# Gated GELU on one core: 8-row tiles with packed output buffers, against 16-row blocks stored from the first load's buffer

## The chip, the core and the metric

The kernel runs on one core of a Trainium2 chip. Of the core's engines three matter here: ScalarE (ACT in the profile) evaluates the GELU, VectorE (DVE) multiplies, and SyncE (SP) computes nothing but issues transfers. ACT issues transfers too. Each of the two has its own queue for them (q1 is SP's, q10 is ACT's in the profile), and both queues are served by the same 16 DMA engines. The metric is device time in microseconds; lower is better. The kernel before was run three times: 469.32, 469.19 and 469.43 us, median 469.32.

## What is computed

```python
def reference(x):                      # x: (32, 512, 2048) float32
    half_dim = x.shape[-1] // 2
    x1, x2 = (x[..., :half_dim].copy(), x[..., half_dim:].copy())
    gelu_x1 = 0.5 * x1 * (1 + erf(x1 / np.sqrt(2)))
    return (gelu_x1 * x2).astype(np.float32)
```

There are 32 x 512 = 16,384 rows of 2048 numbers (8 KB a row). Each gives an output row of 1024 numbers (4 KB). So 134.2 MB are read, 67.1 MB are written, and each element is used once.

## The kernel before, in words

**Tiling.** A tile is 1024 rows: each of the 128 partitions holds R = 8 consecutive rows, so partition p of tile i holds rows 1024 i + 8 p onwards, 64 KB in one piece of DRAM, and its output is 32 KB in one piece (L26 to L29). There are 16 tiles. Two input buffers `x0`, `x1` (64 KB a partition each) and two output buffers `o0`, `o1` (32 KB a partition each) alternate (L30, L31).

**Loads.** All are issued by SP (`load`, L48 to L51). Tile 0 is loaded as two halves of four rows, tile 1 whole; these three wait for nothing (L65 to L69). After tile i has been multiplied, SP issues the load of tile i + 2 into the same input buffer (L113 to L115). It waits only for `mul_done`, not for a store.

**Compute.** For each tile ACT waits until the tile is there (L83, L85), and writes the GELU of the first halves of the rows into the output buffer (L87). DVE waits for ACT and multiplies the output buffer by the second halves, in place (L93 to L100). A tile is done in two steps, rows 0 to 4 and rows 5 to 7; the first and the last tile in three steps of 2, 2 and 4 rows.

**Stores.** ACT issues the store of tile i as soon as DVE has finished it (`store`, L53 to L57); the last two tiles' stores are issued by SP (L105, L110). The load of tile i + 2 and the store of tile i count on one semaphore, `ready[k]`, and ACT waits for both before it overwrites `o[k]`.

**Order.** Everything is written out by hand with counted semaphores. Each queue is a line of its own: what SP issues goes behind what SP issued before, what ACT issues behind what ACT issued before. A small 4 KB transfer to `scrap` opens ACT's queue (L63).

Of the kernel before, what the change touches and what calls it, by code (L numbers as in the profile page):

```python
# [1 line left out]

# [4 lines left out]

GELU = mybir.ActivationFunctionType.Gelu


@with_exitstack
def kernel(
    ctx: ExitStack,
    tc: tile.TileContext,
    x: bass.AP,
    out: bass.AP,
):
    nc = tc.nc
    P = nc.NUM_PARTITIONS

    x_flat = x.flatten_outer_dims()
    out_flat = out.flatten_outer_dims()
    n_rows, dim = x_flat.shape
    half = dim // 2

    R = 8  # L26
    x_t = x_flat.rearrange("(n p r) d -> n p r d", p=P, r=R)
    o_t = out_flat.rearrange("(n p r) d -> n p r d", p=P, r=R)
    n_tiles = x_t.shape[0]  # L29
    x_bufs = [nc.alloc_sbuf_tensor(f"x{k}_tile", [P, R, dim], x.dtype) for k in range(2)]  # L30
    o_bufs = [nc.alloc_sbuf_tensor(f"o{k}_tile", [P, R, half], out.dtype) for k in range(2)]  # L31

    first = [nc.alloc_semaphore(f"first{j}") for j in range(2)]
    ready = [nc.alloc_semaphore(f"ready{k}") for k in range(2)]
    gelu_done = nc.alloc_semaphore("gelu_done")
    mul_done = nc.alloc_semaphore("mul_done")
    tail_stored = nc.alloc_semaphore("tail_stored")
    opened = nc.alloc_semaphore("opened")  # L40
    scrap = nc.alloc_sbuf_tensor("scrap_tile", [8, 128], x.dtype)
    n = {sem.name: 0 for sem in [*first, *ready, gelu_done, mul_done, tail_stored, opened]}

    def counted(ins, sem, by):
        ins.then_inc(sem, by)
        n[sem.name] += by

    def load(i, rows, sem):  # L48
        ins = nc.sync.dma_start(out=x_bufs[i % 2][:, rows, :], in_=x_t[i][:, rows, :])  # L49
        counted(ins, sem, 16)  # L50
        return ins  # L51

    def store(queue, i, rows, sem):  # L53
        queue.wait_ge(mul_done, n[mul_done.name])
        counted(
            queue.dma_start(out=o_t[i][:, rows, :], in_=o_bufs[i % 2][:, rows, :]), sem, 16
        )  # L57

    opening = nc.scalar.dma_start(out=scrap[:, :], in_=x_t[0][:8, 0, :128])  # L63
    counted(opening, opened, 16)
    for ins in (  # L65
        opening,
        load(0, slice(0, 4), first[0]),
        load(0, slice(4, 8), first[1]),
        load(1, slice(0, 8), ready[1]),  # L69
    ):  # L70
        tc.no_tile_sem_insts.add(ins.ins.name)
    tc.close()
    tc.compile()  # L73

    for i in range(n_tiles):
        k = i % 2
        last = i == n_tiles - 1
        pieces = i == 0 or last
        steps = ((0, 2), (2, 4), (4, 8)) if pieces else ((0, 5), (5, 8))
        for lo, hi in steps:  # L80
            rows = slice(lo, hi)
            if i == 0 and lo % 4 == 0:
                nc.scalar.wait_ge(first[lo // 4], 16)  # L83
            elif lo == 0:
                nc.scalar.wait_ge(ready[k], n[ready[k].name])  # L85
            counted(
                nc.scalar.activation(  # L87
                    out=o_bufs[k][:, rows, :], in_=x_bufs[k][:, rows, :half], func=GELU
                ),
                gelu_done,  # L90
                1,
            )
            nc.vector.wait_ge(gelu_done, n[gelu_done.name])  # L93
            counted(
                nc.vector.tensor_mul(  # L95
                    out=o_bufs[k][:, rows, :],
                    in0=o_bufs[k][:, rows, :],
                    in1=x_bufs[k][:, rows, half:],
                ),
                mul_done,  # L100
                1,
            )
            if pieces and hi % 4 == 0:
                if last:
                    store(nc.sync, i, slice(hi - 4, hi), tail_stored)  # L105
                else:
                    store(nc.scalar, i, slice(hi - 4, hi), ready[k])
        if not pieces:
            if i == n_tiles - 2:
                store(nc.sync, i, slice(0, R), tail_stored)  # L110
            else:
                store(nc.scalar, i, slice(0, R), ready[k])
        if i + 2 < n_tiles:  # L113
            nc.sync.wait_ge(mul_done, n[mul_done.name])
            load(i + 2, slice(0, R), ready[k])  # L115


    nc.scalar.wait_ge(opened, 16)
    nc.scalar.drain()  # L119
    for sem in (*first, *ready, opened):  # L120
        nc.scalar.sem_clear(sem)
    nc.vector.drain()
    nc.vector.sem_clear(gelu_done)
    nc.sync.sem_clear(mul_done)
    nc.sync.wait_ge(tail_stored, n[tail_stored.name]).then_inc(
        tail_stored, -n[tail_stored.name]
    )


# [1 line left out]
_INS = ['x']  # L131
_OUTS = [((32, 512, 1024), 'float32')]


# [23 lines left out]
```

## Time and profile before

| what | value |
|---|---|
| median of three runs | 469.32 us (469.19 to 469.43) |
| the profiled execution, first to last event (its span) | 467.8 us |
| what a run's time holds besides (median less span) | 1.5 us |
| DVE busy | 140.5 us, 30% of the span, 34 multiplications |
| ACT busy | 115.5 us, 25%, 34 GELUs and one table load |
| HBM read and written | 134.22 MB and 67.11 MB |
| DMA packets | 5057, mean rate 430 GB/s over the span |

The profiled execution has no time of its own other than its span; the runs of the table were timed around the whole program, 1.5 us more. A duration in the profile is that of one execution. The page's slices cut the span into 40 pieces of 11.7 us, and a digit of 9 in the DMA line means that the 16 DMA engines were busy for 90% of a slice or more. A transfer ("DMA issue") is cut into packets, and the trace records each one's queue, size, start and duration. Here a packet is what one partition gets or gives in one transfer: 64 KB, 32 KB or 16 KB. "Landing" is the time at which a transfer's semaphore has its full count of 16, one from each DMA engine.

### The profile page before, as it was taken

How to read it: one execution, taken by the hardware profiler on the slowest of the kernel's cores; microseconds unless marked ns; L12 is line 12 of the kernel's file. 1: busy time of each engine (PE TensorE's matmuls, PEld its weight loads, DVE VectorE, ACT ScalarE, POOL GpSimd, SP SyncE). 2: the span in 40 equal slices, each digit the busy share in tenths (PEclk: the TensorE clock that was granted, in tenths of full speed). 3: DMA queues.
4: the chain of work that ended last, by engine and by line, in shares of the span. 5: the costliest groups of instructions: out<-in, count | busy, mean ns of one | idle time of the engine just before them, and what ended most of it. 6: DMA issues, size and time to landing. Idle time of an engine off the chain costs nothing.

```text
span 467.8 us, 154 instructions
## 1 busy us (share of the span) xinstructions
DVE 140.5 (30%) x34; ACT 115.5 (25%) x35; POOL 0.2 (0%) x4
## 2 busy tenths in 40 slices
DVE  0330515207051060511606115060150702507043
ACT  1320606041060410604105050050501506014060
POOL 0000000000000000000000000000000000000000
DMA  8999999999999999999999999999999999999988
GB/s 359 448 448 448 398 406 496 403 403 448 459 437 403 440 412 493 403 403 448 487 409 403 445 406 493 403 403 448 493 403 403 448 426 471 403 426 426 493 384 379
DMA packets 5057, 201.34 MB, mean 430 GB/s; under 512 B 568, under 2 KB 576, under 8 KB 576
## 3 DMA queue, kind: packets, MB, share of 16 engines
q1 hardware_dynamic: 2880, 142.61, 70.6%
q10 hardware_dynamic: 2176, 58.73, 29.1%
q14 instruction: 1, 0.01, 0.0%
HBM read 134.22 MB, written 67.11 MB: 430 GB/s over the span
## 4 chain that ended last, share of the span: by engine, by line
DMA 76%; DVE 14%; ACT 8%; ACTq 0%; SPq 0%; issue 0%
DMA out_dram<-o_tile 66%; DVE o_tile L95 14%; DMA x_tile<-in_x_dram 10%; ACT o_tile L87 8%; ACTq L119 0%; SPq L49 0%
## 5 line engine op out<-in xcount | busy, mean ns | idle before, releaser
L95 DVE TENSOR_TENSOR o_tile<-o_tile,x_tile 128x5120 f32<-128x5120 f32 (+3 forms) x34 | 140.5, 4171 | 319.7 <-ACT o_tile L87 319.7
L87 ACT ACTIVATE o_tile<-x_tile 128x5120 f32<-128x5120 f32 (+3 forms) x34 | 114.3, 3407 | 337.3 <-DMA out_dram<-o_tile 301.8
L87 ACT ACT_TABLE_LOAD x1 | 1.3, 1283 | 2.9 <-PEq L73 2.9
L142 POOL MEMSET const-bfloat16-1.0<- 128x1 bf16 x1 | 0.1, 102 | 0.0
L142 POOL MEMSET const-uint8-127<- 128x1 uint8 x1 | 0.1, 101 | 0.0
L142 POOL MEMSET const-float32-0.0<- 128x1 f32 x1 | 0.1, 99 | 0.2 <-issue 0.2
L142 POOL MEMSET const-float32-1.0<- 128x1 f32 x1 | 0.1, 98 | 0.0
## 6 DMA issues: line engine op xcount, KB each, us to landing
out_dram<-o_tile ACTq DMA_DIRECT2D x13, 4096.0 KB, 44.7
x_tile<-in_x_dram SPq DMA_DIRECT2D x2, 4096.0 KB, 16.7
out_dram<-o_tile ACTq DMA_DIRECT2D x2, 2048.0 KB, 34.4
out_dram<-o_tile SPq DMA_DIRECT2D x1, 4096.0 KB, 25.2
out_dram<-o_tile SPq DMA_DIRECT2D x2, 2048.0 KB, 7.8
x_tile<-in_x_dram SPq DMA_DIRECT2D x15, 44.4
scrap_tile<-in_x_dram ACTq DMA_DIRECT2D x1, 4.0 KB
```

The source lines that it names most:

```text
L87: nc.scalar.activation(out=o_bufs[k][:, rows, :], in_=x_bufs[k][:, rows, :half], func=GELU),
L95: nc.vector.tensor_mul(out=o_bufs[k][:, rows, :], in0=o_bufs[k][:, rows, :], in1=x_bufs[k][:, rows, half:],),
L142: nc = _bacc.Bacc("TRN2", target_bir_lowering=False, num_devices=1)
```

## The change: blocks of 16 rows a partition

A block is now 2048 rows, and there are 8 of them. A partition holds a chunk of 16 consecutive rows of the block (128 KB of input, 64 KB of output). The chunk comes in two loads, `h = 0` for its first 8 rows and `h = 1` for its last 8. Each load is 64 KB a partition, as a whole tile was before.

- **Which chunk lies where.** With G = 32 and J = 4, chunk 32 j + g of the block lies in partition 4 g + j. Before, chunk p lay in partition p. So four neighbouring partitions now hold chunks that are 4 MB of input apart, and the next four hold the chunks that follow those.
- **Buffers.** `front[0]` and `front[1]` (64 KB a partition each) take the `h = 0` loads of even and odd blocks; a single `back` (64 KB) takes every `h = 1` load. There is no output buffer.
- **Compute.** ACT writes the GELU over the first halves of the rows, in the buffer in which they were loaded. DVE writes the product packed: that of `h = 0` to the first 32 KB of `front[b % 2]`, over numbers that it has read already, and that of `h = 1`, read from `back`, to the last 32 KB of the same buffer. Before each multiplication DVE now also waits for its own multiplication before that one.
- **Stores.** One store of 64 KB a partition for each block, from `front[b % 2]`, issued by ACT after the block's last multiplication. The last block is stored in three pieces by SP (8, 4 and 4 rows).
- **Loads.** After a block's last multiplication SP issues the `h = 1` load of the next block (`back` is free). Then SP waits until the block's store has landed, and issues the `h = 0` load of the block after next into the buffer that was stored from. At the start three loads are issued without a wait: both halves of block 0 and the first half of block 1. Block 0 is no longer done in small pieces.

The diff's core, with the unchanged counting left out:

```diff
-    x_t = x_flat.rearrange("(n p r) d -> n p r d", p=P, r=R)
-    o_t = out_flat.rearrange("(n p r) d -> n p r d", p=P, r=R)
+    G = 32
+    J = P // G
+    x_t = x_flat.rearrange("(n j g h r) d -> n h g j r d", j=J, g=G, h=2, r=R)
+    o_t = out_flat.rearrange("(n j g r) d -> n g j r d", j=J, g=G, r=2 * R)
...
+    def load(b, h):
+        buf, sem = (front[b % 2], front_moved[b % 2]) if h == 0 else (back, back_loaded)
+        return counted(nc.sync.dma_start(out=buf[:, :], in_=x_t[b, h]), sem, 16)
...
+    def compute(b, h, lo, hi):
+        buf = front[b % 2] if h == 0 else back
+        rows = buf[:, :].rearrange("p (r d) -> p r d", d=dim)[:, lo:hi, :]
+        gelu = rows[:, :, :half]
+        counted(nc.scalar.activation(out=gelu, in_=gelu, func=GELU), gelu_done, 1)
+        if n[mul_done.name]:
+            nc.vector.wait_ge(mul_done, n[mul_done.name])
+        nc.vector.wait_ge(gelu_done, n[gelu_done.name])
+        packed = front[b % 2][:, (h * R + lo) * half : (h * R + hi) * half]
+        counted(
+            nc.vector.tensor_mul(
+                out=packed.rearrange("p (r d) -> p r d", d=half),
+                in0=gelu,
+                in1=rows[:, :, half:],
+            ),
+            mul_done,
+            1,
+        )
...
+    for ins in (opening, load(0, 0), load(0, 1), load(1, 0)):
...
+    for b in range(n_blocks):
+        k = b % 2
+        last = b == n_blocks - 1
+        loaded = 16 + 32 * (b // 2)
+        nc.scalar.wait_ge(front_moved[k], loaded)
+        for lo, hi in ((0, 5), (5, 8)):
+            compute(b, 0, lo, hi)
+        if last:
+            store(nc.sync, b, 0, R, tail_stored)
+        nc.scalar.wait_ge(back_loaded, 16 * (b + 1))
+        if last:
+            for lo, hi in ((0, 2), (2, 4), (4, 8)):
+                compute(b, 1, lo, hi)
+                if hi % 4 == 0:
+                    store(nc.sync, b, R + hi - 4, R + hi, tail_stored)
+        else:
+            for lo, hi in ((0, 5), (5, 8)):
+                compute(b, 1, lo, hi)
             nc.sync.wait_ge(mul_done, n[mul_done.name])
-            load(i + 2, slice(0, R), ready[k])
+            load(b + 1, 1)
+            store(nc.scalar, b, 0, 2 * R, front_moved[k] if b + 2 < n_blocks else tail_stored)
+            if b + 2 < n_blocks:
+                nc.sync.wait_ge(front_moved[k], n[front_moved[k].name])
+                load(b + 2, 0)
```

More of the change, by code (lines that the diff above doesn't have):

```diff
@@ L26 @@
     R = 8
-    x_t = x_flat.rearrange("(n p r) d -> n p r d", p=P, r=R)
-    o_t = out_flat.rearrange("(n p r) d -> n p r d", p=P, r=R)
[L29 to L36, printed above, removed]
+    G = 32
+    J = P // G
+    x_t = x_flat.rearrange("(n j g h r) d -> n h g j r d", j=J, g=G, h=2, r=R)
+    o_t = out_flat.rearrange("(n j g r) d -> n g j r d", j=J, g=G, r=2 * R)
+    n_blocks = o_t.shape[0]
+    front = [nc.alloc_sbuf_tensor(f"a{k}_tile", [P, R * dim], x.dtype) for k in range(2)]
+    back = nc.alloc_sbuf_tensor("b_tile", [P, R * dim], x.dtype)
+    scrap = nc.alloc_sbuf_tensor("scrap_tile", [8, 128], x.dtype)
+    front_moved = [nc.alloc_semaphore(f"front_moved{k}") for k in range(2)]
+    back_loaded = nc.alloc_semaphore("back_loaded")
     gelu_done = nc.alloc_semaphore("gelu_done")
@@ L40 @@
     opened = nc.alloc_semaphore("opened")
-    scrap = nc.alloc_sbuf_tensor("scrap_tile", [8, 128], x.dtype)
-    n = {sem.name: 0 for sem in [*first, *ready, gelu_done, mul_done, tail_stored, opened]}
+    n = {
+        sem.name: 0
+        for sem in [*front_moved, back_loaded, gelu_done, mul_done, tail_stored, opened]
+    }
     def counted(ins, sem, by):
@@ L46, in counted, with store @@
         n[sem.name] += by
-    def load(i, rows, sem):
-        ins = nc.sync.dma_start(out=x_bufs[i % 2][:, rows, :], in_=x_t[i][:, rows, :])
-        counted(ins, sem, 16)
-        return ins
-    def store(queue, i, rows, sem):
+        return ins
+    def load(b, h):
+        buf, sem = (front[b % 2], front_moved[b % 2]) if h == 0 else (back, back_loaded)
+        return counted(nc.sync.dma_start(out=buf[:, :], in_=x_t[b, h]), sem, 16)
+    def store(queue, b, lo, hi, sem):
         queue.wait_ge(mul_done, n[mul_done.name])
         counted(
-            queue.dma_start(out=o_t[i][:, rows, :], in_=o_bufs[i % 2][:, rows, :]), sem, 16
-        )
-    opening = nc.scalar.dma_start(out=scrap[:, :], in_=x_t[0][:8, 0, :128])
-    counted(opening, opened, 16)
[L65 to L70, printed above, removed]
+            queue.dma_start(
+                out=o_t[b, :, :, lo:hi, :], in_=front[b % 2][:, lo * half : hi * half]
+            ),
+            sem,
+            16,
+        )
+    def compute(b, h, lo, hi):
[12 more added lines that the diff above has]
+                in1=rows[:, :, half:],
+            ),
+            mul_done,
+            1,
+        )
+    opening = nc.scalar.dma_start(out=scrap[:, :], in_=x_t[0, 0, :8, 0, 0, :128])
+    counted(opening, opened, 16)
+    for ins in (opening, load(0, 0), load(0, 1), load(1, 0)):
         tc.no_tile_sem_insts.add(ins.ins.name)
@@ L73 @@
     tc.compile()
[L75 to L113, printed above, removed]
-            nc.sync.wait_ge(mul_done, n[mul_done.name])
-            load(i + 2, slice(0, R), ready[k])
@@ L118 @@
     nc.scalar.wait_ge(opened, 16)
     nc.scalar.drain()
-    for sem in (*first, *ready, opened):
+    for sem in (*front_moved, back_loaded, opened):
         nc.scalar.sem_clear(sem)
```

## The prediction

> **What bounds the kernel now.** I read the page's slices and queues first, for whether anything is idle; then the waits and the windows of one steady tile; then the groups, for the work between a landing and the next issue; last the packet records, for what a packet costs.
>
> ```profile
> DVE  0330515207051060511606115060150702507043
> ACT  1320606041060410604105050050501506014060
> DMA  8999999999999999999999999999999999999988
> q1 hardware_dynamic: 2880, 142.61, 70.6%
> q10 hardware_dynamic: 2176, 58.73, 29.1%
> ...
> ACT o_tile L87 <- DMA out_dram<-o_tile: 301.8, 14, 21.9
> ...
> 129.40:158.40 29.00, 8.76 (x2) 7.13 (x3) 0.00 (x0) 1.00 1.00 434
> 158.40:187.40 29.00, 8.76 (x2) 7.12 (x2) 0.00 (x0) 1.00 1.00 434
> ```
>
> The DMA engines are busy throughout: the two queues' packets fill 70.6 + 29.1 = 99.7% of 16 engines' span. ACT's 301.8 us of waiting for stores therefore cost nothing. They are the backlog of a full queue: in a tile's 29.00 us ACT works 7.12 and DVE 8.76 us, and the DMA share (the last three figures are the clock, the share and GB/s) is 1.00. A tile moves 12.58 MB, so 29.00 us is 434 GB/s. The bytes do not change. Only two things can move the time: what a packet costs, and whether the DMA engines ever run dry.
>
> **What a packet costs.** In the packet records, one engine's 64 KB packets follow each other every 2.414 us, its 32 KB packets every 1.2095, its 16 KB packets every 0.607. Two halves take 2.419, 5 ns more than a whole; two quarters also take 5 ns more than a half. So a packet costs about 5 ns beside its bytes. The page's issue rows give the counts:
>
> ```profile
> out_dram<-o_tile ACTq DMA_DIRECT2D x13, 4096.0 KB, 44.7
> x_tile<-in_x_dram SPq DMA_DIRECT2D x2, 4096.0 KB, 16.7
> out_dram<-o_tile ACTq DMA_DIRECT2D x2, 2048.0 KB, 34.4
> out_dram<-o_tile SPq DMA_DIRECT2D x1, 4096.0 KB, 25.2
> out_dram<-o_tile SPq DMA_DIRECT2D x2, 2048.0 KB, 7.8
> x_tile<-in_x_dram SPq DMA_DIRECT2D x15, 44.4
> ```
>
> Each transfer has 128 packets, 8 for each engine. Before: 15 x 8 of 64 KB, (2 + 13 + 1) x 8 of 32 KB, 4 x 8 of 16 KB: 280 an engine. After: 16 loads and 7 stores of 64 KB, one store of 32 KB, two of 16 KB: 184 + 8 + 16 = 208. That saves 72 x 5 ns = 0.36 us, and 9 fewer transfers save 9 completions of 6 ns: **-0.4 us**. By the recorded durations (2.418, 1.213: 8 ns a packet) it would be 0.6, which is the far end.
>
> **Edges.** The first packet starts at 1.74 us in either kernel (SP's first issue is at 0.73). The first 32 KB packets took 1.81 us on average instead of 1.21; I leave these 0.6 us in. Block 0's GELU starts later (after 64 KB a partition, some 22 us, instead of 12.8), which costs nothing: three loads, 58 us of traffic, are queued. The excess of the first 64 KB packets before 60 us, where stores first mix with loads, is 0.38 us an engine. It may recur with the first store or not (0 to -0.4); I leave it in, since that mixing still comes once. At the end, the last loads land with the store of 8 rows (9.7 us of packets) already queued on q1, and 6.4 us later the next store is issued (GELU 1.90, two multiplications 2.29 and 2.25), 4.5 us after that the last: the queue stays filled, as before. Edges: 0.
>
> **Compute.** Same shapes, same counts a byte; in place or not, I take the rows of before (L87: 4.47 and 2.75; L95: 5.49 and 3.35 us). DVE's new wait on itself loses the overlap of its pairs (8.84 in sum, 8.77 on the chain) and some tens of ns: 0.1 to 0.2 us a pair, hidden as long as the queue is filled. ACT's store waits for DVE, and behind it stands the next block's GELU, whose load lands 7 us later (below): nothing waits.
>
> **The new wait is what matters.** Before, a load waited for DVE alone, and a store had 44.7 us to land. Now the load of block b + 2's first half waits for block b's store to land, with SP's queue behind it. I count packets on one engine from L, the end of the load of block b's second half. From there only the next block's first half (8 packets) is queued. ACT starts 0.55 after L (the engines' ends lie 0.25 apart, and the last landing is 0.43 after the last packet's end: 467.375 to 467.80), then 0.02 + 4.48 + 0.02, the chain's 8.77, and 0.1: load and store are issued at L + 13.95. An issue to an idle queue had its first packet 1.01 us later (0.73 to 1.74): L + 14.95. Then the 7th of the 8 packets runs (14.48 to 16.90), the 8th follows to 19.31, and then q1 and q10 alternate packet by packet (loads and stores issued together land together now: 44.4 and 44.7 us). With the store first, its 8th packet ends at 19.31 + 15 x 2.414 = 55.52, and one load packet is left, to 57.94. The landing is at 56.07, SP issues at 56.10, the first new packet is ready at 57.11: **0.8 us to spare**, no idle time, 58 us a block as now. Everything therefore hangs on less than one packet.
>
> So the forecast is 467.8 - 0.4 = 467.4 us of span, and with the 1.5 us that the median holds beside it, **468.9 us**. Its own range is 468.4 to 469.6. A change within 0.2% (0.94 us: 468.4 to 470.3) is what a measurement of this kernel can barely tell from none, so this counts as the same.
>
> **Rival 1, slower: the refill comes late.** If the load's descriptors reach the engines before the store's (SP issues 4 ns earlier and its issue is 34 ns shorter), the load goes first, the store ends at 57.94, and nothing is left behind it: the engines idle 0.55 + 0.03 + 1.01 = 1.6 us. The next load then starts 2.4 + 1.6 = 4.0 us late, which leaves two more packets behind the next store, so the next refill is in time. Of the six refills three pay: 3 x 1.6 = +4.8, **473.7 us**. The same comes by degrees if an issue into a busy queue takes longer than 1.01 us. The trace has one such case: the store issued at 19.26 had its first packet at 24.36, 5.1 us later, past two packets of q1 that began at 20.45 and 21.66. Part of that is turn-taking, but a latency of 2.4 us is allowed by it; then it is 3 x 3.0 = +9 and 478 us. It decides from the point where the store's last packet has less than 1.6 us of load behind it. For it: a margin of 0.8 us in 58. Against it: q10 is the other queue and should have the next turn, and a stall corrects itself in the next block.
>
> **Rival 2, slower: the placement.** Packets now run on other addresses. Before, all 64 KB packets took 2.418 us, whether the engines were in step (first 20 us) or not, so no limit of DRAM shows. The new order puts the chunks of four neighbouring partitions 4 MB apart, and a load's DRAM side is cut in 32 pieces where SBUF's has 128 partitions. If both made two engines share one path at a time, a packet would take up to 2 x 2.418 us and the time would go towards 930 us; a loss of 2% of the rate would already be 9 us. No row of before shows any of it. The Trainium skill, "DMA: Bandwidth & Descriptors", section "Latency and other measured facts", speaks against the change: copies with a pitch between partitions of 4 MiB ran at 103 GB/s a direction, against 207 at 512 KiB and 214 at full rate. By that rule read literally the time would about double. But what counts should be addresses read at one moment by different engines; if each engine has whole groups of four partitions, these are 128 KB apart after, 256 KB before. The same skill's "SBUF — State Buffer", section "Door 1: The DMA port swizzle", has four neighbouring partitions on one port, which fits the groups of four. No run here shows which engine takes which partition.
>
> **Rival 3, faster.** The recorded durations count (0.6 instead of 0.4), and the excess at the first mixing goes with the 16 KB stores that caused it (0.38): -1.0 us, **468.3 us**, just beyond 0.2%. For it: q1's 64 KB packets beside 16 KB ones at 24 to 36 us took up to 0.1 more than 2.418. Against it: packets overlap by 4 ns in the records, and there is no idle time to win.
>
> **Chances.** Forecast 0.45 (same); rival 1 0.30 (470.4 to 478); rival 2 0.08; rival 3 0.17. So faster 0.17, same 0.45, slower 0.38. The range, 467.9 to 476.5 us, takes in the forecast, nearly all of rival 3 and three quarters of rival 1; left out are rival 2 and the far ends, about 0.18.
>
> **What would show it.** Right: DMA digits of 9 in all inner slices, 64 KB packets of 2.418 us in both queues, 58.0 us from one block to the next, SP's wait for the store ending before q1 is empty. Rival 1: gaps of 1 to 3 us without packets after every store or every second one, 62 and 58 us a block in turn. Rival 2: packets well above 2.42 us, with a DMA share still near 1. Rival 3: the sum of the durations 1 us lower an engine. I am wrong altogether if ACT or DVE waits for each other where no transfer is late.

## The result: 5% slower, and what the profile after shows

The changed kernel takes 494.3 us (median of four runs) against 469.35 us before. The ratio is 1.045, with a 95% interval of 1.041 to 1.049. Its runs lie far apart, at 486.9, 493.6, 495.0 and 503.4 us, and the ratio, here and in the first experiment, is formed from the faster two of the four alone. The profiled execution has a span of 492.3 us, 24.5 us more than before. The kernel before spread over 0.2 us.

The page after, first the slices, then the queues; the last line is the GB/s line of before:

```profile
DMA  8999899999999999999999959999999999999998
GB/s 341 442 463 453 346 431 469 453 399 378 426 426 426 421 415 437 426 410 421 362 394 335 367 186 426 426 426 426 426 426 447 447 458 367 399 421 432 431 421 351
...
q1 hardware_dynamic: 2736, 142.61, 69.9%
q10 hardware_dynamic: 1024, 58.72, 27.8%
...
GB/s 359 448 448 448 398 406 496 403 403 448 459 437 403 440 412 493 403 403 448 487 409 403 445 406 493 403 403 448 493 403 403 448 426 471 403 426 426 493 384 379
```

Inside the span one slice has a 5 and one an 8 where before had nines, but the rest looks busy, and that is the trap of this line. The GB/s line shows more: 335 to 394 in six slices whose DMA digit is 9, where no such slice of before has less than 398. An engine can be busy with a packet that takes too long. The queues' shares add up to 97.7%, not 99.7%.

The table of stretches by block shows where the time went. Each window runs from one store that ACT issues to the next. The second column is its length; the last three are clock, DMA share and GB/s.

```profile
55.88:114.89 59.01, 17.70 (x4) 14.24 (x4) 0.00 (x0) 1.00 1.01 425
114.89:175.22 60.33, 17.70 (x4) 14.24 (x4) 0.00 (x0) 1.00 0.99 416
175.22:236.68 61.46, 17.70 (x4) 14.25 (x4) 0.00 (x0) 1.00 1.01 424
236.68:304.65 67.97, 17.70 (x4) 14.25 (x4) 0.00 (x0) 1.00 0.90 342
304.65:366.90 62.25, 17.70 (x4) 14.25 (x4) 0.00 (x0) 1.00 1.00 423
366.90:425.02 58.12, 17.70 (x4) 14.24 (x4) 0.00 (x0) 1.00 1.00 430
```

The forecast was 58.0 us for every block. One block has it (58.12). The others take 1 to 10 us more, with the same compute and, in most, a full DMA share. The waits of SP's queue name the new dependency (two lines of after, then one of before):

```profile
SPq L55 <- DMA out_dram<-a_tile: 268.6, 6, 54.1
SPq L55 <- DVE a_tile L77: 146.2, 7, 52.2
...
SPq L49 <- DVE o_tile L95: 396.5, 14, 29.4
```

SP now waits six times for a store to land before it may load again (first line). Before, its loads waited for DVE alone (last line).

The packet records say what happens at these six places. I call the load that waits for the store the refill. "First packet" is how much longer than 2.418 us each the packets took that end within 8 us of the refill's issue (nearly all of it falls on the refill's first packet), "before the store" the same for the load packets that end within 8 us of the issue of ACT's next store. Both are sums for one engine, as a mean over the 16.

| refill issued (us) | its first packets start | first packet | before the store |
|---|---|---|---|
| 98.93 | 1.3 to 2.1 us later | +0.49 | +1.12 |
| 159.29 | 1.3 to 3.6 | +0.58 | +1.19 |
| 218.88 | 1.5 to 4.0 | +0.47 | +1.22 |
| 291.33 | 1.3 to 1.9 | +0.69 | +1.18 |
| 348.58 | 3.8 to 4.4 | 0.00 | +0.03 |
| 409.05 | 1.3 to 3.8 | +0.62 | +1.16 |

The refill of 348.58 found all engines still busy with queued packets, and its block shows neither delay. In the other five the earliest packets started 1.3 to 1.5 us after the issue. By then some or all engines had stood idle in four of the five; in the first (98.93) none had, since the packets in progress ended just as the new ones came. On top, after 236.68 the load packets went on being stretched for a whole block (6.9 us an engine, 1.2 of them the table's), the 16 engines fell up to 5.8 us apart, and twelve of those that had finished stood idle for 5 to 8 us until the slowest had written its share of the store: that is the 5 in the DMA line. Summed over the span, packets took 16.6 us an engine more than their usual durations (before: 1.0), the time that they left of the span grew by 9.5 us, and fewer packets saved 0.6 by their recorded durations: 15.6 + 9.5 - 0.6 = 24.5 us, the measured difference.

### The profile page after: what moved, and what is told of

Read it like the earlier page. It is cut to its first block, busy times and chain, and to the rows that moved or that the text cites. A ratio compares the mean times of both kernels' runs of the same rounds, so it can differ in the third digit from the quotient of the medians.

```text
span 492.3 us, 174 instructions
## 1 busy us (share of the span) xinstructions
DVE 141.8 (29%) x33; ACT 115.3 (23%) x34; POOL 0.2 (0%) x4
## 4 chain that ended last, share of the span: by engine, by line
DMA 70%; DVE 12%; ACT 8%; another core or an unknown queue 8%; ACTq 0%; issue 0%; SPq 0%; DVEq 0%
DMA b_tile<-in_x_dram 56%; DVE a_tile L77 12%; DMA out_dram<-a_tile 9%; ACT b_tile L71 7%; DMA a_tile<-in_x_dram 6%; ACT a_tile L71 1%; ACTq L119 0%; SPq L55 0%; DVEq L74 0%
## 5 line engine op out<-in xcount | busy, mean ns | idle before, releaser
L77 DVE TENSOR_TENSOR a_tile<-b_tile 128x5120 f32<-128x5120 f32 (+3 forms) x17 | 71.0, 4174 | 202.2 <-ACT b_tile L71 201.9
L77 DVE TENSOR_TENSOR a_tile<-a_tile 128x5120 f32<-128x5120 f32 (+1 forms) x16 | 70.8, 4425 | 140.6 <-ACT a_tile L71 140.4
L71 ACT ACTIVATE b_tile<-b_tile 128x5120 f32<-128x5120 f32 (+3 forms) x17 | 57.1, 3407 | 217.8 <-DMA b_tile<-in_x_dram 217.8
L71 ACT ACTIVATE a_tile<-a_tile 128x5120 f32<-128x5120 f32 (+1 forms) x16 | 57.0, 3608 | 143.2 <-DMA a_tile<-in_x_dram 143.2
```

Source lines behind the costliest of these rows:

```text
L71: counted(nc.scalar.activation(out=gelu, in_=gelu, func=GELU), gelu_done, 1)
L77: nc.vector.tensor_mul(out=packed.rearrange("p (r d) -> p r d", d=half), in0=gelu, in1=rows[:, :, half:],),
```

## Experiments

Four theories were tested, two of them formed on the way. **Placement**: the new DRAM addresses make packets slow. **Second queue**: waking ACT's empty queue beside SP's running one costs the microsecond. **Near-empty queue**: it costs when new packets arrive at a queue with one or two left. **Dry engines**: what costs is that the engines reach the end of what is queued before the refill is there. The first four expectations still take the last three together as 'drained queue'.

### The changed kernel with the old placement

```diff
-    x_t = x_flat.rearrange("(n j g h r) d -> n h g j r d", j=J, g=G, h=2, r=R)
-    o_t = out_flat.rearrange("(n j g r) d -> n g j r d", j=J, g=G, r=2 * R)
+    x_t = x_flat.rearrange("(n p h r) d -> n h p (r d)", p=P, h=2, r=R)
+    o_t = out_flat.rearrange("(n p r) d -> n p r d", p=P, r=2 * R)
```

> The changed kernel with chunk p in partition p, as before (16-row chunks, 128 KB apart from partition to partition); buffers, waits and queues stay as changed. Theory 'placement' (the new DRAM addresses make packets slow: 64 KB packets of SP's queue took 2.535 us on average instead of 2.418): the packets return to 2.42 us and the time to 468 to 471 us. Theory 'drained queue' (what costs is that both queues run nearly empty once a block: the packet in progress when a new transfer arrives is stretched by about 1 us, refills come late, engines fall out of step): the time stays where the changed kernel is, 485 to 503 us, with stretched packets 3 to 7 us after each pair of issues.

Measured: 484.4 to 495.0 us in four runs, median 489.8; ratio 1.034 (1.032 to 1.036). The same picture: five refills whose first packets took 0.24 to 1.17 us more, each followed by +0.87 to +1.47 before the next store, and one refill in time (0.00, then +0.03). Its slices:

```profile
DMA  9999999999999999999999999999689999999998
```

The 6 is again one block with engines that wait for the slowest. Placement is not the cause.

### The kernel before with the new placement

```diff
-    x_t = x_flat.rearrange("(n p r) d -> n p r d", p=P, r=R)
-    o_t = out_flat.rearrange("(n p r) d -> n p r d", p=P, r=R)
+    x_t = x_flat.rearrange("(n j g r) d -> n g j r d", j=4, g=32, r=R)
+    o_t = out_flat.rearrange("(n j g r) d -> n g j r d", j=4, g=32, r=R)
```

> The kernel before with only the placement changed: 8-row tiles, chunk 32j+g in partition 4g+j, for loads and stores. Placement: packets above 2.42 us, 475 to 495 us. Drained queue: this kernel's queues always hold a backlog, so all packets take 2.418 and 1.213 us and the time is that of before, 468.5 to 470.5 us.

Measured: 469.8 us, ratio 1.0011 (1.0002 to 1.0020). Two tiles of it, then the rows of SP's load issues, first of before (L49), then of this kernel (minimum, median and maximum duration in ns):

```profile
114.37:143.38 29.01, 8.76 (x2) 7.12 (x2) 0.00 (x0) 1.00 1.00 434
143.38:172.37 28.99, 8.76 (x2) 7.12 (x2) 0.00 (x0) 1.00 1.00 434
```

```profile
L49 SPq DMA_DIRECT2D x_tile<-in_x_dram x17: 327/328/425, 0.7 to 403.7; - x17
```

```profile
L49 SPq DMA_DIRECT2D x_tile<-in_x_dram x17: 534/535/663, 0.7 to 404.4; - x17
```

A tile still takes 29.0 us, so the addresses cost nothing here. The chunks are half as long as in the changed kernel, so those of neighbouring partitions lie 2 MB apart, not 4. For copies with such a pitch the Trainium skill ("DMA: Bandwidth & Descriptors", "Latency and other measured facts") gives 164 GB/s a direction at 2 MiB and 103 at 4 MiB, against 214 at full rate. Neither loss is seen, 434 GB/s here and as much at 4 MB in the kernel with the store in two halves below; only four partitions at a time lie so far apart in these kernels. What the placement costs is a longer issue, 0.54 instead of 0.33 us and 0.66 instead of 0.38 for the first, which delays the first packets.

### One queue, store first

```diff
+            store(nc.sync, b, 0, 2 * R, front_moved[k] if b + 2 < n_blocks else tail_stored)
             load(b + 1, 1)
-            store(nc.scalar, b, 0, 2 * R, front_moved[k] if b + 2 < n_blocks else tail_stored)
```

> The changed kernel with the block's store issued by SP ahead of the next second-half load, instead of by ACT behind it: one queue, in order. The store then lands about 19 us before the queue is empty, so no refill is late and no second queue is woken. Placement: packets stay slow, the time stays above 480 us. Drained queue: no idle gaps and no engine out of step; if the stretching comes from waking ACT's empty queue it is gone too and the time is 467 to 470 us; if it comes from any issue into a queue with one or two packets left, about 7 times 1 us stay, 474 to 477 us.

Measured: 473.2 us (472.5 to 473.4), ratio 1.008 (1.006 to 1.010). SP's wait for stores:

```profile
SPq L55 <- DMA out_dram<-a_tile: 146.1, 6, 24.9
```

It has fallen from 268.6 to 146.1 us, because the store goes ahead of the load. The first store shows +0.96 us; at the later ones, with one or two packets left in the queue as before, it is 0.02 to 0.18. So near-empty is not enough to cause the stretch. What is left, 4 us, is compared with the control's below.

### Half-size blocks, refill two blocks later

```diff
-    R = 8
+    R = 4
-    front = [nc.alloc_sbuf_tensor(f"a{k}_tile", [P, R * dim], x.dtype) for k in range(2)]
-    back = nc.alloc_sbuf_tensor("b_tile", [P, R * dim], x.dtype)
+    front = [nc.alloc_sbuf_tensor(f"a{k}_tile", [P, R * dim], x.dtype) for k in range(4)]
+    back = [nc.alloc_sbuf_tensor(f"b{k}_tile", [P, R * dim], x.dtype) for k in range(2)]
...
+            if 0 <= b - 1 and b + 3 < n_blocks:
+                j = (b - 1) % 4
+                nc.sync.wait_ge(front_moved[j], n[front_moved[j].name])
+                load(b + 3, 0)
```

> The changed scheme with half-size blocks (8 rows a partition, 32 KB loads and 32 KB stores, four front and two back buffers in the same memory): a front load still waits for its buffer's store, but two blocks later, so both queues keep a backlog. New placement, packed stores, DVE's self-wait and in-place GELU all stay. 176 more packets an engine at 5 ns are +0.9 us. Placement: stays slow, above 475 us. Drained queue: 468 to 471 us, no stretched packets after the first block, no idle time.

Measured: 479.8 us, ratio 1.023 (1.020 to 1.026). The time is one that placement had named, but the two experiments above rule placement out; 'drained queue' had expected 468 to 471 us and missed. The engines are never idle before the end (4.5 us in the last 20 us, before 0.7), but load packets in front of most of ACT's stores after the first take 0.0 to 0.5 us more, 5.2 us in all with the first store's 1.0 and the start. ACT's queue had run empty before most of these stores, so waking it may cost something without any late refill; this run does not isolate that.

### Control and waking by itself

Before, with all stores on SP's queue ahead of the load; then the same with one tiny load on ACT's otherwise empty queue after each store.

```diff
-                store(nc.scalar, i, slice(0, R), ready[k])
+                store(nc.sync, i, slice(0, R), ready[k])
+                nc.scalar.wait_ge(mul_done, n[mul_done.name])
+                counted(nc.scalar.dma_start(out=small[:, i * 128 : (i + 1) * 128],
+                    in_=x_t[i][:16, 0, :128]), woken, 16)
```

> The kernel before with all stores issued by SP ahead of the load (one queue, always with a backlog). Control for the next run. Theory 'second queue' (the stretch of about 1 us comes from waking ACT's empty queue beside SP's running one) and theory 'near-empty queue' (it comes whenever descriptors arrive at engines that have only one or two packets left, in whichever queue) both expect the time of before, 469 to 470 us, without stretched packets after the first 30 us.

> The same, and after each of 13 stores ACT issues one small load (16 x 512 B, one packet an engine, 0.025 us each) on its own queue, which is empty every time: 13 wakings beside a deep SP queue. It adds work that the output does not need. Second queue: 13 stretched packets of 0.5 to 1.2 us an engine, 476 to 485 us. Near-empty queue: SP's queue is deep, so 469 to 471 us and no stretch.

Measured: 474.2 us (1.011, 1.009 to 1.013) and 474.1 us (1.011, 1.009 to 1.013). Thirteen wakings by a tiny load cost nothing; a waking as such is not the price. But the control is 5 us slower than before, which neither theory had expected: the first store costs 1.55 us, packets are stretched by 0.0 to 0.2 us a tile, and the engines end up to 1.6 us apart, with 3.4 us of idle time in the last 20 us (before: 0.7). The one-queue kernel above has much the same (first store 0.96, idle time at the end 2.9), so its 4 us are most likely the price of one queue, not of the blocks.

### One queue, load first: a late refill by construction

```diff
-            store(nc.scalar, b, 0, 2 * R, front_moved[k] if b + 2 < n_blocks else tail_stored)
+            store(nc.sync, b, 0, 2 * R, front_moved[k] if b + 2 < n_blocks else tail_stored)
```

> The changed kernel with the store issued by SP behind the next second-half load: one queue, and by construction nothing behind the store when it lands. Late refill is now certain in all six blocks: 0.55 to the landing, 0.03, 1.0 to the first packet, about 1.6 us idle, and 0.5 us for the first packet after it: 6 x 2.1 = 13 us. Near-empty queue: the pair of issues still meets SP's queue with one or two packets left, 7 x 1.1 = 8 us, so 469 + 13 + 8 = about 490 us. Second queue: no second queue is woken, so without those 8 us, about 482 us.

Measured: 494.9 us (494.9 to 495.1), ratio 1.055 (1.053 to 1.057). Slices and wait:

```profile
DMA  8999999989999899997999979989899998999998
```

```profile
SPq L55 <- DMA out_dram<-a_tile: 344.8, 6, 60.6
```

Six dips of one slice lie at the six refills (a seventh, the 8 at 321 to 333 us, does not). The time is beyond both expectations. Every block pays 2.2 to 2.6 us of idle time, 0.6 to 0.8 on the first packet, and 1.0 to 1.2 on the load packet before the next store's first packet, although that store is on the same queue with nothing to wake and comes some 37 us later. That is 4.0 us a block and 24 in all; the kernel with only the order of store and load exchanged was 21.8 us faster. This run made the theory of dry engines: the last microsecond belongs to the drained engines, not to a queue.

### The store in two halves

```diff
-        if last:
-            store(nc.sync, b, 0, R, tail_stored)
+        kept = front_moved[k] if b + 2 < n_blocks else tail_stored
+        store(nc.sync if last else nc.scalar, b, 0, R, kept)
...
-            store(nc.scalar, b, 0, 2 * R, front_moved[k] if b + 2 < n_blocks else tail_stored)
+            store(nc.scalar, b, R, 2 * R, kept)
```

> The changed kernel with each block's store in two (32 KB a partition each): ACT issues the first half's store as soon as the first half is multiplied, 20 us before the other. The second part is 8 packets of 1.21 us, so it lands about 10 us before SP's queue is empty and the refill is in time; ACT's queue is woken twice a block, beside a deep SP queue the first time. Late refills gone: no idle time and engines in step, runs within 1 us of each other. Near-empty queue: stretch once a block, about 7 us: 474 to 477 us. Second queue: stretch twice a block, 14 us: 481 to 485 us.

Measured: 471.0 us (470.8 to 471.5), ratio 1.004 (1.002 to 1.006). Two blocks:

```profile
58.32:116.36 58.04, 17.70 (x4) 14.24 (x4) 0.00 (x0) 1.00 1.01 435
116.36:175.07 58.71, 17.70 (x4) 14.24 (x4) 0.00 (x0) 1.00 1.00 435
```

Packet records: +1.07 us at the first store, then 0.00 to 0.01 at every issue of ACT. After the first store ACT's queue is not woken in this kernel: each half is issued before the last has landed. So this run does not speak against 'second queue'. The store issued at 366.90 in the trace after does: ACT's queue had been without a packet for 21 us, and the store cost 0.03 us. With the refill early enough, 23 of the 25 us are gone and so is the spread between runs, with placement, in-place compute, DVE's wait on itself and the wait for the store all kept.

### The changed kernel once more

> The changed kernel once more, for a second trace of it, since its runs lie 16 us apart. Theory 'dry engines' (formed from the runs so far: whenever the DMA engines reach the end of what is queued before the refill's packets are there, the block pays the idle time, about 0.6 us on the first packet after it, and about 1.1 us on the load packets in front of the next store; a refill that is in time pays none of the three): every late refill shows all three, every refill in time shows none, and together they account for all but 2 us of the distance to before. Rivals 'second queue' and 'near-empty queue': the 1.1 us stands at every store of ACT, whatever the refill before it did.

Measured: 501.4 us, span 500.0. The last four blocks of it:

```profile
176.06:238.80 62.74, 17.70 (x4) 14.25 (x4) 0.00 (x0) 1.00 0.99 418
238.80:305.36 66.56, 17.70 (x4) 14.25 (x4) 0.00 (x0) 1.00 0.91 348
305.36:368.41 63.05, 17.70 (x4) 14.25 (x4) 0.00 (x0) 1.00 1.02 431
368.41:431.33 62.92, 17.70 (x4) 14.25 (x4) 0.00 (x0) 1.00 0.87 368
```

Five refills are late (+0.42 to +0.80, then +0.95 to +1.38 before the next store), one is in time (0.00, then +0.01). Over the two traces of the changed kernel, that with the old placement and the one-queue kernel with the load first, that makes 21 late refills with the second delay and 3 in time without. But the three prices leave about 7 of the 32 us to before open, not the 2 us expected, most of it in two blocks whose packets were stretched turn after turn. One is the block from 238.80 (5.4 us an engine). The other, from 368.41, is the one whose refill was in time, and it still lost 5 us: two engines had packets of loads and store stretched to as much as 3.7 us, and the fourteen others stood idle for 6 to 9 us until these had finished the store. The first trace has one such block. Of the 7.7 us between the two spans the block from 368.41 makes 4.8; what sets the other runs apart no trace shows.

### A head start for the store

```diff
-            nc.sync.wait_ge(mul_done, n[mul_done.name])
-            load(b + 1, 1)
             store(nc.scalar, b, 0, 2 * R, front_moved[k] if b + 2 < n_blocks else tail_stored)
+            nc.scalar.wait_ge(mul_done, n[mul_done.name])
+            idle = back[:, : 8 * half]
+            counted(nc.scalar.activation(out=idle, in_=idle, func=GELU), paused, 1)
+            nc.sync.wait_ge(paused, n[paused.name])
+            nc.sync.wait_ge(mul_done, n[mul_done.name])
+            load(b + 1, 1)
```

> The changed kernel, but SP issues the next second-half load about 7 us after ACT's store: in between ACT runs one extra 128x8192 GELU in the free back buffer, which nothing uses, and SP waits for it. The store then has two or three packets ahead of the load, so it lands some 5 us before SP's queue is empty. Placement, 64 KB packets, both queues, and the waking of ACT's empty queue once a block stay as in the changed kernel. Dry engines: every refill in time, no idle time and no stretched packet after the first store: 469 to 471.5 us. Second queue or near-empty queue: the seven wakings still cost 1.1 us each, 476 to 479 us.

Measured: 474.2 us (472.2 to 475.6), ratio 1.010 (1.007 to 1.013), between the two. ACT's queue is woken seven times: +1.07 at the first store, 0.00 at the second, then 0.12 to 0.59, 1.9 us in all for the six after the first. The refills' first packets started 2.1 to 4.5 us after the issue, and single engines stood idle for up to 1.6 us. Most of the loss is gone, as dry engines would have it; the remainder has no settled cause. The wakings by themselves are not it: the second store met an empty queue like the others.

### Two halves with the old placement

> The changed kernel with the store in two halves and chunk p in partition p: the refill is in time, and SP's issues are 0.2 us shorter. If the two placements differ only by that, 470.3 to 471.0 us against 470.99 for the same with the new placement; before's 469.3 is not reached, because the first store still costs 1.1 us where before's small first stores cost 0.4.

The edits are those of the first and of the two-halves experiment together. Measured: 470.5 us (470.4 to 470.8), ratio 1.0027 (1.0018 to 1.0037). Two blocks:

```profile
57.84:115.84 58.00, 17.70 (x4) 14.25 (x4) 0.00 (x0) 1.00 1.00 434
115.84:173.82 57.98, 17.70 (x4) 14.24 (x4) 0.00 (x0) 1.00 1.01 436
```

These are the 58.0 us of the forecast; the next two blocks took 58.83 and 58.11. Half a microsecond less than with the new placement would agree with the shorter issues, but the two intervals overlap. The kernel before stays the fastest: no version made here beats it.

## Why the prediction was wrong, step by step

- **What bounds the kernel, and the packet's price: right.** Undisturbed 64 KB packets take 2.418 us in all kernels, in both queues and at both placements. The 0.4 us to be gained is too small to be seen beside the rest.
- **Edges: too low.** The first store costs 1.0 us of stretched packets; before's small first stores cost 0.4, and I had left it at no difference. The first packet starts at 2.18 us, not at 1.74 as in the kernel before: the new placement's longer issue adds the 0.5 us of the second experiment.
- **Compute: right.** DVE's pairs take 8.88 instead of 8.77 us, and load and store of block 0 are issued at 55.88, some 14.0 us after the load's end; I had 13.95.
- **The step that failed: "0.8 us to spare, no idle time".** I had the landing at 1.9 us before the end of the old packets. In block 0 the store landed at 98.93 and the old packets ended at about 100.65, 1.7 us later, but that this agrees is luck: two errors cancelled. The store's last 64 KB packets ended at 95.43 to 96.18, so the landing took 2.7 us, not 0.55. Each engine closes its share of a transfer with a 4-byte packet, and here that packet (97.84 to 98.59) came 2.41 us after the last 64 KB packet, behind one more load packet. Against that, two load packets were left behind the store's last one and not one, because the store's first two packets ran back to back.

  What the step had wrong in its result is what a refill needs. I took 1.01 us from the very first issue of the kernel before. With the new placement, whose load issues are 0.2 us longer, idle engines had a refill's first packet 1.32 us after the issue at the earliest; with the old placement it was 0.96, and the refills were late all the same. The larger error is that just in time is already too late. In block 0 no engine was idle, and yet the first packets took 0.49 us more and those before the next store 1.12. Refills whose earliest packet started 2.1 to 2.9 us after the issue (head start) showed a part of this, up to 0.15 and 0.59 us. Those in which no engine's started before 3.1 us showed at most 0.03, where ACT issues the stores of whole-size blocks. The Trainium skill ("DMA: Bandwidth & Descriptors", "Anatomy of one DMA") gives about 2.0 us of fixed cost for a transfer, there for descriptors written by software. The traces' own sum for the two ends of a transfer, 0.43 from the last packet to the landing and 1.32 or 0.96 from issue to packet, is 1.8 us at the new placement and 1.4 at the old, below that figure.
- **Rival 1 named the mechanism and was sized at a fifth.** It priced a late refill at its idle time, 1.6 us. The runs show three prices: the idle time, about 0.6 us for the first packet, and about 1.1 us before the next store. I had seen the 0.6 us at the start of the program and "left it in" without charging it to any refill. And the wait is for the slowest of 16 engines: once they fell out of step, up to 8 us went in a single block. A stall did correct itself in the next block, as I had argued, but only a long one: the three refills in time (348.58 here, one in the second trace, one with the old placement) each follow the refill before which the engines had stood idle for some 5 us. In the first trace three load packets were left behind the last packet of the store issued at 304.65, and two in block 0 and after the shorter stalls.
- **Rival 2: refuted** by the first two experiments, and by the two halves, which have the new placement and 58.04 us a block. **Rival 3:** nothing of it was seen.

What stays open: why drained engines pay a second time at the next store, up to 40 us later, why some engines' packets are then stretched turn after turn, and what the 0.1 to 0.6 us at ACT's stores are where no refill was late (half blocks, head start).

## What to carry to other kernels

Where the DMA engines are the bound, a load that waits for a store's landing must have more than the time from issue to first packet queued behind that landing on every engine: here 3.1 us was enough, 2.1 to 2.9 was partly too little, 1.7 was too little. Count it from the landing on the slowest engine to the end of the queue on the engine that is first done; allow for a packet of the other queue ahead of the landing; and charge a dry moment with its after-effects, 1.7 us here, as well as with its idle time. Cutting the store so that most of it is gone before the critical moment bought that cover for 5 ns a packet and brought 23 of 25 us back. A DMA digit of 9 does not mean full rate: read the GB/s beside it.

## What the runs showed of the hardware

- A store issued into an empty queue beside a running one had its first packet some 5 to 7 us later, on most engines after two more 64 KB packets of the other queue had started (first trace of the changed kernel); a refill of idle engines needed 1.32 us, with the old placement 0.96.
- The 4-byte packet that closes a store's share on an engine came 2.41 us after its last 64 KB packet, behind a load packet (block 0 of the changed kernel, and nearly every later block).
- The same traffic on one queue instead of two cost 5 us in the kernel before (474.2 against 469.2), more than half of it idle time at the end.
- With 32 DRAM pieces against 128 partitions an issue took 0.54 us instead of 0.33; the rate of the transfer was the same, 434 GB/s.
